# Gates of tiles 1 to 3 moved behind the attention, gates and output projection on operands in two parts

## The chip, the cores and the metric

One core of a Trainium2 chip runs the program. The metric is the device time of one execution in microseconds (us); a lower one is better. The kernel before takes 2186.17 us, the median of three runs (2179.91 to 2187.29). A difference of about 0.3%, some 6.6 us, is what a measurement of this kernel can tell from none.

## The reference, cut to what matters

Two layers follow each other on 512 tokens of width 1024. The first mixes two kinds of attention through gates, then adds a layer of experts that are looked up per token; the second is a state-space layer. The change lies in the first:

```
h = rmsnorm(x, norm1_g); proj = h @ w_in
qa, ka, va, qb, kb, vb, ga, gb = split(proj)
ya = neighbourhood_attention(qa, ka, va, rpb)          # 8 heads of 64
yb = gqa_attention(rope(norm(qb)), rope(norm(kb)), vb) # 8 heads of 64, 2 key heads
merged = sigmoid(ga) * (ya @ w_proj_a) + sigmoid(gb) * (yb @ w_proj_b)
x = x + merged @ w_out
x = x + peer(rmsnorm(x, norm2_g))     # per token 128 rows of peer_u and peer_v, 16 for each of 8 heads
...                                   # then the second layer
```

`ga` and `gb` are 1024 wide each, so the gates are two products of 512x1024 by 1024x1024. The kernel uses sigmoid(a) = (tanh(a/2) + 1) / 2. `peer` picks for each token and head 16 of 16384 experts by two rankings, and weights their rows.

## The kernel before

The tokens are four tiles of 128. Tile 0 goes first through attention, gates and output (`mix_first`), and its experts are ranked (`queries`, `ranked`, `best`). Tiles 1 to 3 then go together, 384 tokens wide, through `mix_rest`: `mixers` runs 24 units (2 kinds of attention, 4 pairs of heads, 3 tiles), and each unit is scores `s`, a softmax on VectorE and ScalarE, transposes `pT` and the weighted sum `y`. `beside(u)` is called behind each unit and, in this kernel, `spread` computes one 128-wide piece of a gate in it: pieces of `ga` behind units 0 to 7 (into `mT`), of `gb` behind units 12 to 19 (into the tile `gb`). `merge` then multiplies the attention's output `yT` by `wproj` (tile `pj`), multiplies it with the gates (L681, L682) and projects with `wout` (tile `xo`, L688). All of this is in fp32: a matmul of fp32 operands shows as two records in the trace.

The experts are the other half of the program. For each of the 4 x 128 experts of a tile's tokens, GpSimd gathers 128 rows of 8 KB (`uv`, L273) into one of six buffers `g`, VectorE multiplies and sums (L275), ScalarE applies Gelu (L280), VectorE builds a diagonal `dg` (L284) and, for tile 0, adds half of the output itself in `own` (L299, with L293), and TensorE adds the rest into `acc` (L289). A buffer `g` is free for the next gather when `acc` and `own` have read it. These steps are issued by a generator (`peers`) of two gathers a step: `Paced` counts the columns of every matmul (four for each fp32 column, one for one of fp32r) and, each time PACE columns have been issued, lets the generator take one step. PACE_B holds during `mix_rest` and the queries of tile 1, PACE_Q and PACE_C afterwards. The generator for tile 1 waits for the ranking of tile 1, which needs the result of `mix_rest`.

A scheduler then fixes the order on each engine. Each engine runs its instructions in that order, so what stands ahead of an `acc` on TensorE, or ahead of an L275 on VectorE, holds it up. After `mix_rest` come the queries of tile 1 (`pq`, `sc`) with a ranking behind each of four steps, then the queries and rankings of tiles 2 and 3, then the second layer for tiles 0 and 1 beside the last gathers, and for tiles 2 and 3 when all gathers are done.

Other places of the program already use operands in two parts: `halves` splits a weight tile into `ww`, a rounded fp32r part (a ScalarE cast, L357) and the rest (a VectorE subtraction, L358), and PARTS makes three fp32r products of it, high by high, high by low and low by high, each one record in the trace:

```
PARTS = ((0, 0), (0, 1), (1, 0))
A.copy(ww[:, 0], w)
V.tensor_tensor(ww[:, 1], w, ww[:, 0], op=OP.subtract)
```

Of the kernel before, what the change touches and what calls it, by code (L numbers as in the profile page):

```python
# [8 lines left out]
F32 = mybir.dt.float32  # L9
F32R = mybir.dt.float32r  # L10
# [4 lines left out]
OP = mybir.AluOpType  # L15
# [158 lines left out]
def program(tc, a, out):  # L174
# [2 lines left out]
    T = Paced(nc.tensor)  # L177
    first, rest = [0], [1, 2, 3]
    NG = 256
    PACE_B, PACE_Q, PACE_C = 15000, 10500, 4600  # L180

    with ExitStack() as ctx:
        cst = ctx.enter_context(tc.tile_pool(name="cst", bufs=1))
# [14 lines left out]
        def bank(name, tag="mm"):  # L198
            if tag in turns:
                turn[tag] = turn.get(tag, -1) + 1  # L200
                tag = turns[tag][turn[tag] % len(turns[tag])]
            return ps.tile([P, 512], F32, tag=tag, name=name, bufs=2 if tag in ("mm", "sb") else 1)

        def wtile(src, n):
            t = wp.tile([P, 1024 // n, n], F32, tag="w", name="w")
            SP.dma_start(t, src)
            return t
# [183 lines left out]
        with pool("pa") as pa:  # L391
# [28 lines left out]
            with pool("ph") as ph:  # L420
# [76 lines left out]
                def mix_rest(tiles, hs):  # L497
                    n = len(tiles) * P
                    with pool("p2") as py:
                        yT = py.tile([P, 8, n], F32, tag="yT", name="yT")  # L500
                        mT = py.tile([P, 8, n], F32, tag="mT", name="mT")
                        gb = []

                        def gate(i, w, dst):
                            b = bank("ga")
                            rows(w[i], hs, b, n)
                            A.activation(dst[:, i, :], b[:, :n], AF.Tanh, scale=0.5)

                        def spread(u):

                            if u < 8:
                                gate(u, a["wga"], mT)
                            if 12 <= u < 20:
                                if not gb:
                                    gb.append(pa.tile([P, 8, n], F32, tag="kv", name="gb"))
                                gate(u - 12, a["wgb"], gb[0])

                        def put(i, b):
                            A.copy(yT[:, i, :n], b[:, :n])

                        with pool("p2a", 2) as pw:
                            mixers(pw, tiles, hs, put, spread)
                        merge(tiles, yT, mT, gb[0])

                def mix_first(hs, hl):

# [142 lines left out]
                            weigh(*units[u - ahead])  # L669
                            beside(u - ahead)  # L670

                def merge(tiles, yT, mT, gb):
                    n = len(tiles) * P
                    for d in range(8):
                        w = wtile(a["wproj"][d], P)
                        sg = mT[:, d, :], gb[:, d, :]
                        for j, o in enumerate(sg):
                            b = bank("pj", "sb")
                            for k in range(4):
                                T.matmul(b[:, :n], w[:, 4 * j + k, :], yT[:, 4 * j + k, :n], start=(k == 0), stop=(k == 3))  # L680
                            V.scalar_tensor_tensor(o, o, 1.0, b[:, :n], op0=OP.add, op1=OP.mult)  # L681
                        V.tensor_tensor(sg[0], sg[0], sg[1], op=OP.add)  # L682
                    for half in range(2):
                        bs = [bank("xo") for _ in tiles]
                        cols(bs, mT, [(i, a["wout"][half, i]) for i in range(4)])
                        for i, t in enumerate(tiles):
                            xs = xres[:, t, half * 512:(half + 1) * 512]
                            V.scalar_tensor_tensor(xs, bs[i], 0.5, xs, op0=OP.mult, op1=OP.add)  # L688
# [463 lines left out]
```

## Time and profile before

| | us |
|---|---|
| median of three runs | 2186.17 |
| the profiled execution | 2190.49 |
| its span, first to last instruction | 2188.6 |
| TensorE busy (10292 matmul records) | 1817.3 |
| VectorE busy | 1625.2 |
| ScalarE busy | 736.3 |
| GpSimd busy (512 gathers) | 590.6 |

The profiled execution is 4.3 us above the median, and 1.9 us of it lie around the span. Its program can be cut by places that every reader finds again: the units of `mixers` for tiles 1 to 3 run from about 293 us (the first gate product) to 610 us (the last `y`), `merge` until 711 us, the queries and rankings of tile 1 until 795 us, those of tiles 2 and 3 until about 1130 us; the last gather lands at about 1905 us, and what follows is the second layer of tiles 2 and 3 alone. A busy share is the busy time of an engine over a stretch. A wait names the engine and line that waited and what ended the wait.

### The profile page before, as it was taken

The page shows a single profiled execution, that of the slowest core. Times are in us where ns is not written, and L with a number is a line of the kernel's source. Part 1 is how long each engine was busy: PE and PEld are TensorE (multiplying, and loading weights), DVE is VectorE, ACT ScalarE, POOL GpSimd, SP SyncE. Part 2 cuts the span into 40 slices and gives each one's busy share as a digit, 9 for nine tenths or more (in the row PEclk, how much of TensorE's full clock was granted, in tenths as well). Part 3 has the DMA queues.
Part 4 walks back from the last instruction along what each step waited for, and adds up shares of the span by engine and source line. Part 5 has one row for each costly group of instructions (what it writes and reads, how often), then busy time and mean ns, then how long its engine had stood idle before and what let it go on. Part 6 is the DMA issues. An engine that isn't in the chain of part 4 may idle for free.

```text
span 2188.6 us, 29527 instructions
## 1 busy us (share of the span) xinstructions
PE 1817.3 (83%) x10292; PEld 1030.6 (47%) x10292; DVE 1625.2 (74%) x4007; ACT 736.3 (34%) x1471; POOL 590.6 (27%) x520
## 2 busy tenths in 40 slices
PE   7898779989999799555567987896899866699998
PEld 5666534444443765011114653462463311189996
DVE  5376987788786685998877887886775756688865
ACT  4364256566500431111122342421220310144543
POOL 0000232333332133443433334333433334200000
PEclk9999889999999899666678997897899976699999
DMA  6366979889897989999998999899999999743453
GB/s 215 111 215 218 365 274 348 345 330 363 336 376 271 340 339 382 421 408 395 410 389 317 418 363 407 329 418 420 402 415 418 414 369 421 328 152 120 136 191 116
DMA packets 127316, 711.71 MB, mean 325 GB/s; under 512 B 15168, under 2 KB 18752, under 8 KB 61248
## 3 DMA queue, kind: packets, MB, share of 16 engines
q0 software_dynamic: 73728, 536.90, 60.8%
q1 hardware_dynamic: 53440, 172.92, 22.6%
q8 instruction: 83, 1.36, 0.2%
q14 instruction: 65, 0.53, 0.1%
HBM read 707.67 MB, written 2.10 MB: 324 GB/s over the span
## 4 chain that ended last, share of the span: by engine, by line
PE 34%; DVE 26%; DMA 23%; ACT 8%; issue 6%; POOL 1%; another core or an unknown queue 0%; SPq 0%; DVEq 0%; ACTq 0%; POOLq 0%
DMA g<-in_uv,idx 20%; DVE g L275 10%; PE sc L168 6%; PE acc L289 4%; PE mix L168 4%; PE pq L168 3%; DVE dg L284 2%; PE z L168 2%; DVE own L299 2%; DVE ww L358 2%; PE pg L168 2%; PE xbc L168 2%; ACT L280 2%; POOL g L273 1%; PE xo L168 1%
## 5 line engine op out<-in xcount | busy, mean ns | idle before, releaser
L273 POOL DMA_INDIRECT g<-in_uv,idx x512 | 586.8, 1146 | 1290.6 <-PE acc L289 636.5
L289 PE MATMUL acc<-g,dg 64*64 64x512 f32 x3584 | 606.7, 748 | 242.6 <-DVE dg L284 214.1
L275 DVE SCALAR_TENSOR_TENSOR g<-g,xnp 128x1024 f32<-128x1024 f32 x512 | 625.1, 1221 | 179.5 <-DMA g<-in_uv,idx 177.3
L289 PEld LDWEIGHTS acc<-g,dg 64*64 64x64 f32 x3584 | 126.8, 156 | 589.8 <-DVE dg L284 428.2
L280 ACT ACTIVATE act<-act 128x1 f32<-128x1 f32 (+1 forms) x448 | 90.9, 203 | 922.7 <-DVE g L275 893.2
L358 DVE TENSOR_TENSOR ww<-w,ww 128x1024 fp32r<-128x1024 f32 x175 | 213.5, 1223 | 82.7 <-ACT ww L357 81.2
L284 DVE TENSOR_SCALAR dg<-two,act,gate 128x64 f32<-128x64 f32 x512 | 169.8, 349 | 118.9 <-ACT act L280 109.9
L357 ACT CAST ww<-w 128x1024 fp32r<-128x1024 f32 x175 | 182.1, 1045 | 162.1 <-PE sc L168 46.8
L168 PEld LDWEIGHTS sc<-hT,ww 128*128 128x128 f32 x1536 | 192.4, 195 | 54.5 <-issue 43.8
L168 PE MATMUL sc<-hT,ww 128*128 128x256 f32 x1536 | 209.2, 292 | 5.5 <-ACT fold L337 3.3
L168 PE MATMUL pq<-xT,w 128*128 128x128 f32 (+1 forms) x768 | 124.2, 320 | 4.7 <-ACT q L736 3.8
L168 PEld LDWEIGHTS pq<-xT,w 128*128 128x128 f32 x768 | 111.8, 198 | 18.3 <-ACT q L736 5.5
L299 DVE SCALAR_TENSOR_TENSOR own<-g,hid,own 128x512 f32<-128x512 f32 x127 | 95.2, 750 | 2.3
L168 PE MATMUL ga<-h,w 128*128 128x384 f32 x256 | 92.5, 511 | 2.4 <-DVE rot L415 2.4
L280 ACT ACT_TABLE_LOAD x60 | 77.0, 1283 | 16.0 <-DVE g L275 13.0
L168 PE MATMUL xbc<-hT,ww 128*128 128x256 f32 x480 | 65.0, 292 | 11.1 <-ACT ww L357 5.7
L168 PEld LDWEIGHTS xbc<-hT,ww 128*128 128x128 f32 x480 | 59.9, 194 | 25.6 <-issue 8.6
L168 PEld LDWEIGHTS ga<-h,w 128*128 128x128 f32 x256 | 48.4, 197 | 36.9 <-issue 7.8
L168 PE MATMUL q<-h,w 128*128 128x128 f32 (+1 forms) x256 | 60.8, 392 | 4.2 <-ACT rsq L411 4.2
L168 PE MATMUL mix<-w,ycat 128*128 128x512 f32 x128 | 61.7, 612 | 0.0
L168 PEld LDWEIGHTS z<-hT,ww 128*128 128x128 f32 x384 | 46.9, 190 | 12.2 <-issue 10.5
L168 PEld LDWEIGHTS q<-h,w 128*128 128x128 f32 x256 | 40.5, 198 | 23.9 <-ACT rsq L411 4.8
(337 smaller groups left out, 2256.2 us busy)
## 6 DMA issues: line engine op xcount, KB each, us to landing
w<-in_w SPq DMA_DIRECT2D x100, 512.0 KB
w<-in_wq SPq DMA_DIRECT2D x48, 512.0 KB
w<-in_wo SPq DMA_DIRECT2D x32, 512.0 KB
w<-in_wgm SPq DMA_DIRECT2D x16, 512.0 KB
w<-in_wout SPq DMA_DIRECT2D x16, 512.0 KB
g<-in_uv,idx POOLq DMA_INDIRECT x512
w<-in_wpg SPq DMA_DIRECT2D x16, 512.0 KB
w<-in_wqa SPq DMA_DIRECT2D x8, 512.0 KB
```

The costliest lines, as they stand in the source:

```text
L168: return self.count(max(n, 128) * (4 if rhs.dtype == F32 else 1), self.tensor.matmul(out, lhsT, rhs, **kw))
L273: G.indirect_dma_start(out=g.rearrange("p a d -> p (a d)"), out_offset=None, in_=a["uv"], in_offset=bass.IndirectOffsetOnAxis(ap=hk_idx[t] ...
L275: V.scalar_tensor_tensor(g[:, 0, :], g[:, 0, :], 1.0, xnp, op0=OP.mult, op1=OP.mult, accum_out=act[:, j % grp:j % grp + 1])
L280: A.activation(act[:, :grp], act[:, :grp], AF.Gelu)
L284: V.tensor_scalar(dg[:, m, :], two[:, 1, :], act[:, m:m + 1], gate[:, m:m + 1], op0=OP.mult, op1=OP.mult)
L289: T.tensor.matmul(acc[i][o, :], w, v, start=(e0 + j + 1 == grp), stop=(e0 + j + grp >= P), tile_position=(64 * i, 64 * m), skip_group_chec ...
L299: V.scalar_tensor_tensor(own, g[:, 1, HALVES[1]], hid[:, j:j + 1], own, op0=OP.mult, op1=OP.add)
L357: A.copy(ww[:, 0], w)
L358: V.tensor_tensor(ww[:, 1], w, ww[:, 0], op=OP.subtract)
```

## The change

`spread`, `gate` and the tile `gb` go. `mixers` gets an empty function for `beside`, so its units follow one another with nothing between but the steps of the experts. `merge` gets the normed input `hs` and does more:

- `parts` splits `hs` (8 pieces of 128x384: a cast on ScalarE, a subtraction on VectorE) into `hp` and `hpl`, and later the merged `mT` into `mp` and `mpl`. The low parts lie in the tile of the keys and values, the high parts in a pool that opens when the pool of `mixers` has closed.
- For each of eight pieces `d`, both gates are computed by `halves` and PARTS (2 x 24 fp32r matmuls of 384 columns), tanh goes into two small tiles `sg`, and `wproj` is used as before.
- `wout` is split by `halves` too (8 tiles), and 144 fp32r matmuls of 512 columns take the place of 48 fp32 ones; the three accumulators `xo` lie in banks of two kinds (`mm`, `sb`).
- PACE_B is 13700 and was 15000. By Paced's count, `mix_rest` had 798,720 columns and has 724,992 now, so 53.2 steps of the generator and now 52.9; but `mixers` had 602,112 of them and has 405,504 now, 40.1 steps and now 29.6.

The weights that are loaded, the gathers and all the rest are the same.

```diff
--- before.py
+++ after.py
@@ -177,7 +177,7 @@
     T = Paced(nc.tensor)
     first, rest = [0], [1, 2, 3]
     NG = 256
-    PACE_B, PACE_Q, PACE_C = 15000, 10500, 4600
+    PACE_B, PACE_Q, PACE_C = 13700, 10500, 4600
 
     with ExitStack() as ctx:
         cst = ctx.enter_context(tc.tile_pool(name="cst", bufs=1))
@@ -498,29 +498,13 @@
                     n = len(tiles) * P
                     with pool("p2") as py:
                         yT = py.tile([P, 8, n], F32, tag="yT", name="yT")
-                        mT = py.tile([P, 8, n], F32, tag="mT", name="mT")
-                        gb = []
-
-                        def gate(i, w, dst):
-                            b = bank("ga")
-                            rows(w[i], hs, b, n)
-                            A.activation(dst[:, i, :], b[:, :n], AF.Tanh, scale=0.5)
-
-                        def spread(u):
-
-                            if u < 8:
-                                gate(u, a["wga"], mT)
-                            if 12 <= u < 20:
-                                if not gb:
-                                    gb.append(pa.tile([P, 8, n], F32, tag="kv", name="gb"))
-                                gate(u - 12, a["wgb"], gb[0])
-
                         def put(i, b):
                             A.copy(yT[:, i, :n], b[:, :n])
 
                         with pool("p2a", 2) as pw:
-                            mixers(pw, tiles, hs, put, spread)
-                        merge(tiles, yT, mT, gb[0])
+                            mixers(pw, tiles, hs, put, lambda u: None)
+                        with pool("p2m", 2) as pm:
+                            merge(pm, tiles, yT, hs)
 
                 def mix_first(hs, hl):
 
@@ -669,20 +653,48 @@
                             weigh(*units[u - ahead])
                             beside(u - ahead)
 
-                def merge(tiles, yT, mT, gb):
+                def merge(pm, tiles, yT, hs):
+
                     n = len(tiles) * P
+
+                    def parts(src, name):
+                        hi = pm.tile([P, 8, n], F32R, tag="hi", name=name, bufs=1)
+                        lo = pa.tile([P, 8, n], F32R, tag="kv", name=name + "l")
+                        for k in range(8):
+                            A.copy(hi[:, k, :], src[:, k, :])
+                            V.tensor_tensor(lo[:, k, :], src[:, k, :], hi[:, k, :], op=OP.subtract)
+                        return hi, lo
+
+                    hp = parts(hs, "hp")
+                    mT = ph.tile([P, 8, n], F32, tag="h2", name="mT")
                     for d in range(8):
+                        sg = []
+                        for j, src in enumerate((a["wga"], a["wgb"])):
+                            w = halves(pm, wtile(src[d], P))
+                            b = bank("ga")
+                            for k in range(8):
+                                for x, y in PARTS:
+                                    T.matmul(b[:, :n], w[:, x, k, :], hp[y][:, k, :], start=(k + x + y == 0), stop=(k == 7 and x == 1))
+                            o = pm.tile([P, n], F32, tag=f"sg{j}", name="sg")
+                            A.activation(o, b[:, :n], AF.Tanh, scale=0.5)
+                            sg.append(o)
                         w = wtile(a["wproj"][d], P)
-                        sg = mT[:, d, :], gb[:, d, :]
                         for j, o in enumerate(sg):
                             b = bank("pj", "sb")
                             for k in range(4):
                                 T.matmul(b[:, :n], w[:, 4 * j + k, :], yT[:, 4 * j + k, :n], start=(k == 0), stop=(k == 3))
                             V.scalar_tensor_tensor(o, o, 1.0, b[:, :n], op0=OP.add, op1=OP.mult)
-                        V.tensor_tensor(sg[0], sg[0], sg[1], op=OP.add)
+                        V.tensor_tensor(mT[:, d, :], sg[0], sg[1], op=OP.add)
+                    mp = parts(mT, "mp")
                     for half in range(2):
-                        bs = [bank("xo") for _ in tiles]
-                        cols(bs, mT, [(i, a["wout"][half, i]) for i in range(4)])
+                        bs = [bank("xo", "mm" if i < 2 else "sb") for i in range(len(tiles))]
+                        for m in range(4):
+                            w = halves(pm, wtile(a["wout"][half, m], 512))
+                            for i, b in enumerate(bs):
+                                for j in range(2):
+                                    for x, y in PARTS:
+                                        T.matmul(b, mp[x][:, 2 * m + j, i * P:(i + 1) * P], w[:, y, j, :],
+                                                 start=(m + j + x + y == 0), stop=(m == 3 and j == 1 and x == 1))
                         for i, t in enumerate(tiles):
                             xs = xres[:, t, half * 512:(half + 1) * 512]
                             V.scalar_tensor_tensor(xs, bs[i], 0.5, xs, op0=OP.mult, op1=OP.add)
```

The order on each engine shifts with it. On TensorE, in the middle of `mixers` (kind 0: `s` scores, `pT` transposes, `y` weighted sums, `acc` the experts), before:

```order
L168 MATMUL y<-pT,kv 64x128
L168 MATMUL ga<-h_1502,w 128x384 x8
L168 MATMUL s<-kv,qT 128x512
L168 MATMUL y<-pT,kv 64x128 x7
L171 MATMUL pT<-idn,s 128x128 x4
L289 MATMUL acc<-g,dg 64x512 x2
```

and in the changed kernel:

```order
L168 MATMUL y<-pT,kv 64x128
L171 MATMUL pT<-idn,s 128x128 x4
L168 MATMUL s<-kv,qT 128x512 x2
L168 MATMUL y<-pT,kv 64x128 x7
L171 MATMUL pT<-idn,s 128x128 x4
L168 MATMUL s<-kv,qT 128x512
L289 MATMUL acc<-g,dg 64x512 x4
```

The gate products are gone from between the units. Two `acc` belong to a gather of tile 0. Ahead of the last `y` stood 200 of them, 100 gathers, and stand 160 now, 80 gathers; ahead of the last `xo` stood all 256, and stand 208 now, 104 gathers.

On VectorE, in the middle of `merge`, before (L681 and L682 are the merging):

```order
L682 TENSOR_TENSOR mT<-mT,gb 128x384
L681 SCALAR_TENSOR_TENSOR mT<-mT,pj 128x384
L275 SCALAR_TENSOR_TENSOR g,act<-g,xnp 128x1024
L284 TENSOR_SCALAR dg<-two,act,gate 128x64 x2
L293 TENSOR_TENSOR hid<-act,gate 128x2
L299 SCALAR_TENSOR_TENSOR own<-g,hid,own 128x512
L275 SCALAR_TENSOR_TENSOR g,act<-g,xnp 128x1024
L299 SCALAR_TENSOR_TENSOR own<-g,hid,own 128x512
L681 SCALAR_TENSOR_TENSOR gb<-gb,pj 128x384
```

and in the changed kernel (L686 and L687 are the merging now, L358 the split of a weight tile):

```order
L687 TENSOR_TENSOR mT<-sg 128x384
L358 TENSOR_TENSOR ww<-w,ww 128x1024 x2
L686 SCALAR_TENSOR_TENSOR sg<-sg,pj 128x384 x2
L687 TENSOR_TENSOR mT<-sg 128x384
L358 TENSOR_TENSOR ww<-w,ww 128x1024 x2
L686 SCALAR_TENSOR_TENSOR sg<-sg,pj 128x384
L275 SCALAR_TENSOR_TENSOR g,act<-g,xnp 128x1024
```

The experts' work has left the middle of `merge`: on TensorE no `acc` stands between the 72nd and the 264th gate product.

On VectorE, in the first ranking of tile 1 (MAX, MAX_INDEX and MATCH_REPLACE find the largest scores), before:

```order
L774 TENSOR_TENSOR cand<-v_4793 128x2x56
L747 MATCH_REPLACE sc<-v_4793,sc 128x128 x4
L748 MAX v_4793<-sc 128x8 x4
L749 MAX_INDEX i_4794<-v_4793,sc 128x8 x3
L777 TENSOR_TENSOR cand<-v_4793 128x2x8
```

and in the changed kernel:

```order
L786 TENSOR_TENSOR cand<-v_5272 128x2x56
L759 MATCH_REPLACE sc<-v_5272,sc 128x128
L275 SCALAR_TENSOR_TENSOR g,act<-g,xnp 128x1024
L759 MATCH_REPLACE sc<-v_5272,sc 128x128
L299 SCALAR_TENSOR_TENSOR own<-g,hid,own 128x512
L759 MATCH_REPLACE sc<-v_5272,sc 128x128 x2
L760 MAX v_5272<-sc 128x8 x2
```

Work on the last gathers of tile 0 has moved in between. From the last `xres` of `mix_rest` (L688) to the last indices of tile 1 (L812) VectorE handled 10 gathers, and handles 30 now; at those indices both orders stand at gather 138, and both go on alike from there.

## Rows read from the trace of the kernel before

**Rows 1.** Page, part 4: share of the span by engine, then by line, in the chain.
```profile
PE 34%; DVE 26%; DMA 23%; ACT 8%; issue 6%; POOL 1%; another core or an unknown queue 0%; SPq 0%; DVEq 0%; ACTq 0%; POOLq 0%
DMA g<-in_uv,idx 20%; DVE g L275 10%; PE sc L168 6%; PE acc L289 4%; PE mix L168 4%; PE pq L168 3%; DVE dg L284 2%; PE z L168 2%; DVE own L299 2%; DVE ww L358 2%; PE pg L168 2%; PE xbc L168 2%; ACT L280 2%; POOL g L273 1%; PE xo L168 1%
```

**Rows 2.** Busy time by stretch: us, busy us per engine, clock, DMA share, GB/s.
```profile
core 0: us, PE busy (x) PEld busy (x) DVE busy (x) ACT busy (x) POOL busy (x), PEclk, DMA share, GB/s
250.00:300.00 50.00, 34.51 (x114) 15.37 (x113) 48.21 (x200) 18.84 (x35) 14.02 (x10) 0.73 0.82 311
293.00:610.00 317.00, 292.53 (x1411) 143.29 (x1411) 247.88 (x553) 188.61 (x324) 102.34 (x89) 0.99 0.88 337
409.00:455.00 46.00, 35.86 (x218) 17.31 (x218) 37.80 (x83) 30.07 (x52) 16.43 (x15) 1.00 0.85 335
610.00:711.00 101.00, 94.75 (x328) 41.25 (x324) 75.11 (x151) 4.58 (x19) 26.67 (x24) 1.00 0.83 324
711.00:795.00 84.00, 70.08 (x478) 57.76 (x479) 65.90 (x331) 32.19 (x66) 20.41 (x18) 0.90 0.89 336
862.00:1120.00 258.00, 149.75 (x818) 31.89 (x810) 228.19 (x751) 37.56 (x139) 114.80 (x100) 0.68 0.99 408
```

**Rows 3.** Waits, 293 to 706 us: engine line waited for: us, times, longest us.
```profile
POOL g L273 <- PE acc L289: 192.2, 33, 13.7
...
DVE g L275 <- DMA g<-in_uv,idx: 44.6, 31, 3.7
```

**Rows 4.** GpSimd in order of time: start us, us, operation [idle before <-releaser].
```profile
686.12 1.43 POOL L273 DMA_INDIRECT g<-in_uv,idx  x1 [0.30 <-issue]
741.54 0.94 POOL L273 DMA_INDIRECT g<-in_uv,idx  x1 [53.99 <-issue]
```

**Rows 5.** TensorE in order of time: last mixing product, first query product behind.
```profile
609.41 1.09 PE L168 MATMUL y<-pT,vb 128*64 128x128 f32 x16
...
711.80 0.39 PE L168 MATMUL pq<-xT,w 128*128 128x128 f32 x2
```

**Rows 6.** VectorE in order of time: last indices of tile 1.
```profile
795.39 0.18 DVE L812 CAST idx<-idxf 128x32 int32<-128x32 f32 x1
```

**Rows 7.** Lines by shape, 293 to 706 us: xcount | busy us, mean ns | idle before.
```profile
L275 DVE SCALAR_TENSOR_TENSOR g<-g,xnp 128x1024 f32<-128x1024 f32 x115 | 140.3, 1220 | 44.6 <-DMA g<-in_uv,idx 44.6
...
L168 PE MATMUL ga<-h,w 128*128 128x384 f32 x256 | 92.5, 511 | 2.4 <-DVE rot L415 2.4
L299 DVE SCALAR_TENSOR_TENSOR own<-g,hid,own 128x512 f32<-128x512 f32 x118 | 88.5, 750 | 2.3
L289 PE MATMUL acc<-g,dg 64*64 64x512 f32 x468 | 74.0, 611 | 9.3 <-DVE dg L284 7.5 <-DVE hid L293 1.8
...
L168 PE MATMUL pj<-yT,w 128*128 128x384 f32 x128 | 44.0, 494 | 3.0 <-DVE gb L681 3.0
...
L284 DVE TENSOR_SCALAR dg<-two,act,gate 128x64 f32<-128x64 f32 x116 | 31.9, 336 | 29.4 <-ACT act L280 28.3 <-issue 1.0
...
L275 DVE DVE_READ_ACCUMULATOR g<-g,xnp 128x1 f32 x115 | 9.6, 84 | 0.0
L293 DVE TENSOR_TENSOR hid<-act,gate 128x2 f32<-128x2 f32 x58 | 9.1, 157 | 0.0
```

**Rows 8.** Lines by shape, 1950 to 2150 us, where operands are in two parts.
```profile
L168 PE MATMUL sc<-hT,ww 128*128 128x256 f32 x768 | 96.2, 285 | 0.0
...
L358 DVE TENSOR_TENSOR ww<-w,ww 128x1024 fp32r<-128x1024 f32 x59 | 72.2, 1224 | 29.0 <-ACT ww L357 28.6
L357 ACT CAST ww<-w 128x1024 fp32r<-128x1024 f32 x58 | 60.7, 1046 | 71.6 <-PE sc L168 33.4 <-PE mix L168 19.0 <-issue 11.7
L168 PE MATMUL mix<-ww,yc 128*128 128x512 f32 x180 | 41.6, 393 | 0.0
```

## The prediction

> **What bounds the kernel now.** I read the chain first [rows 1]: no engine holds more than a third of it, TensorE 34%, VectorE 26%, transfers 23%, and the longest single item is the landing of gathers, 20%. So the program is a long queue of gathers, and what matters is how fast the rest lets them go. Busy time by stretch says which engine that is [rows 2]. From 293 to 610 us, where the change takes its gates out, TensorE is busy 292.53 of 317 us, 92%; VectorE 78%, ScalarE 59%. From 610 to 711 us, the merging, TensorE is busy 94%. From 862 to 1120 us it is VectorE, 88%, with the DMA engines at 0.99. The waits say how the gathers hang on this [rows 3]: GpSimd waited 192.2 us for an `acc` on TensorE to free a buffer, while VectorE waited 44.6 us for gathers. TensorE is thus the bound in front, but VectorE is close behind. One hole stands out: the last gather of tile 0 is issued at 686.12 us, the next one at 741.54 us, when tile 1's first indices are there [rows 4]. I cut the program at the last `y` (610 us), the first query product of tile 1 (711 us) [rows 5] and tile 1's last indices (795 us) [rows 6]. At the last of these both orders stand at gather 138, so what the change costs up to there should be what it costs in all: behind it the work is the same, with the DMA engines full until 1120 us, and I see nothing that gives time back.
>
> **What a gather of tile 0 costs.** On VectorE 1220 + 84 + 336 + 750 + half of 157 ns, 2.47 us. On TensorE two `acc` of two records, 74.0 us for 468 records being 158 ns each, 0.63 us [rows 7].
>
> **First stretch, the attention.** The change takes out the gates, 256 records and 92.5 us of TensorE [rows 7], and the order takes out 20 gathers (80 instead of 100 ahead of the last `y`). TensorE falls from 292.5 to 292.5 - 92.5 - 12.6 = 187 us. VectorE falls from 247.9 by 20 x 2.47 to 198.5 us. TensorE is then no longer the bound; without gates to fill in, softmax, transposes and experts wait for each other, and VectorE is the longest. The trace holds a piece of such work: from 409 to 455 us no gate product but those at its end ran, and VectorE was busy 82%, TensorE 78% [rows 2]. There the experts came thicker, so I take 85%: 198.5 / 0.85 = 233.5 us instead of 317, a gain of 83.5 us. Its bounds are 78%, VectorE's share in this stretch now (254 us, a gain of 63), and 88%, that of 862 to 1120 us (224.5 us, a gain of 92.5). [...]
>
> **Second stretch, the merging.** It was 101 us. The gates arrive, 384 fp32r products of 384 columns. The trace has such products of 256 columns, 96.2 us for 768, 125 ns, and of 512, 41.6 us for 180, 231 ns [rows 8]; I take the middle, 178 ns, 68.4 us, with 48 and 89 us as bounds. `wproj` took 44.0 us for 64 products [rows 7], of which 56 stand behind the last `y`, 38.5 us. The output becomes 144 products of 231 ns, 33.3 us. With 24 gathers of 0.63 us, 15.1 us, TensorE has 155 us. In front of it the split of `hs` must run, which can begin only when the pool of `mixers` is closed: 8 pieces that no row shows, at most 1.22 us each like a whole split [rows 8] and at least nothing for all but the first; I take 5 us. In the output VectorE has eight splits of 1.22 us and ten gathers, 34.5 us, with the low parts of `mT` and the additions to `xres` on top, as much as TensorE's 33.3 + 6.3 us, and a split that stands behind a gather waits for its landing; I take 8 us, between 0 and 20. That makes 168 us, 67 us more. The rest is covered: 24 weight splits are 24 x 1.05 = 25 us on ScalarE, which was busy 4.58 of 101 us here, and 24 x 1.22 = 29 us on VectorE, which with 24 gathers (59 us) stays far under 168. If that cover failed, each gate would wait about 2.3 us, 37 us for 16. The 16 weight tiles of the gates change their place on SP's queue too: 8.4 MB at the 408 GB/s of 862 to 1120 us [rows 2] are 21 us, beside 24 gathers, which came at 258 / 100 = 2.58 us each from 862 us on, 62 us; the DMA engines have room. But gathers starve here: no `acc` stands between the 72nd and 264th gate product.
>
> **Third stretch, tile 1's rankings.** VectorE was busy 65.9 of 84 us [rows 2]. The 20 gathers that were left behind come here, 49.4 us, so it has 115.3 us. At 88%, its share from 862 us on, where rankings and gathers also mix, that is 130 us, 46 us more. Were it never idle, 31 us more; at the share it has here now, 78%, 63 us more. The gathers fill the hole after 686 us, which helps the DMA engines, but VectorE was at work in it.
>
> **The sum.** -83.5 + 67 + 46 = +29.5 us on the profiled execution's 2190.5 us, 2220 us; that execution was 4.3 us over the median, so 2216 us. In words: TensorE saves some 35 us of products, VectorE gets 24 x 1.22 us and the small splits more, and work that lay side by side is put into one stretch that only TensorE fills and one that only VectorE fills.
>
> **Rivals.** *VectorE packs (faster).* With fewer gathers among the units and none of tile 0 waiting behind gates, VectorE could run at the 96% of 250 to 300 us [rows 2], 48.21 of 50 us, in the first and third stretch. Then they take 207 and 120 us, gains and costs of 110 and 36; with the 13 us of waits in the merging gone too (54 us more) the sum is -20 us, 2166 us. It gets faster by over 0.3% from a share of 92%: (198.5 + 115.3) / 0.92 = 341, 60 us under the 401 now, against 54. For it speaks that VectorE's idle time is mostly waits for gathers (44.6 us) which come thinner; against it that at 96% nothing of attention ran beside.
> *It comes out even.* The 20 gathers first fill the 18 us in which VectorE is idle in the third stretch, and it is then never idle (31 us more); the attention runs at 88% (a gain of 92.5), the merging at half its waits (61 us more). Sum 0, 2186 us.
> *The clock falls.* If the attention gets the 0.73 of 250 to 300 us, TensorE needs 187 / 0.73 = 257 us there, and at its own 92% of now 278 us, 44.5 us more than forecast: 2260 us. For it speaks the row at 69% busy, against it the one at 78%; the forecast has TensorE at 187 / 233.5 = 80%.
>
> **How the numbers follow.** The forecast has 0.53: it rests on two counted sums and on shares of VectorE of which this trace has nearby examples. Packing 0.22, even 0.13, the clock 0.12. Some 0.3%, 6.6 us, is what can be told from no change. Slower: nearly all of the forecast (0.49) and the clock, 0.61. Faster: nearly all of packing and a rest of the forecast, 0.23. Within: 0.16. By its bounds the forecast goes from -92.5 + 54 + 31 = -7 us to -63 + 87 + 63 = +87 us; its ends need all bounds at once. The range from 2172 to 2250 us takes in the even case and most of packing, and leaves out the clock case and packing's far end.
>
> **What would show it.** In the profile of the changed kernel the last `y` should end near 527 us, the first query product of tile 1 start near 695, tile 1's last indices come near 825. VectorE should be busy about 85% up to the last `y`, TensorE over 90% in the merging, VectorE about 88% in the rankings, and gathers should be few in the merging and without a hole behind it. A gate product should take near 178 ns. The prediction is wrong if the attention ends before about 505 us, if the rankings cost under 35 us more, or if the shift at the last indices is not the shift at the end.

## The result, and the profile after

The changed kernel takes 2220.5 us, the median of six runs (2211.49 to 2222.79), beside 2186.73 us for the kernel before on the same chip: a ratio of 1.0155, 95% interval 1.0136 to 1.0174. The forecast was 2216 us, slower. The profiled execution of the changed kernel took 2222.79 us, its span is 2221.0 us, 32.4 us more than before.

The chain of waits, page part 4 (shares of the span by engine, then by line), answers to [rows 1]: still no engine above some 36%, and transfers of gathers the longest item.

```profile
PE 36%; DVE 24%; DMA 20%; issue 9%; ACT 8%; POOL 2%; POOLq 0%; SPq 0%; DVEq 0%; ACTq 0%
DMA g<-in_uv,idx 18%; DVE g L275 9%; PE sc L168 6%; PE acc L289 4%; PE ga L168 3%; POOL g L273 2%; PE mix L168 2%; DVE dg L284 2%; PE z L168 2%; PE pj L168 2%; PE pg L168 2%; DVE ww L358 2%; PE xo L168 2%; ACT L280 2%; PE xbc L168 2%
```

The three places at which the prediction cut the program, in order of time: the last `y` and the end of the output on TensorE, tile 1's last indices on VectorE [rows 5, 6].

```profile
529.58 1.09 PE L168 MATMUL y<-pT,vb 128*64 128x128 f32 x14
...
694.64 0.39 PE L168 MATMUL xo<-ww,mpl 128*128 128x512 f32 x1
...
817.06 0.17 DVE L824 CAST idx<-idxf 128x32 int32<-128x32 f32 x1
```

The busy time by stretch, cut there, answers to [rows 2] (columns as there: us, busy us and instructions of each engine, granted clock, DMA share, GB/s). The last two rows cut the whole program at 1150 us.

```profile
core 0: us, PE busy (x) PEld busy (x) DVE busy (x) ACT busy (x) POOL busy (x), PEclk, DMA share, GB/s
293.00:531.00 238.00, 208.05 (x1068) 96.52 (x1066) 197.64 (x449) 173.99 (x293) 76.69 (x68) 0.92 0.86 318
531.00:695.00 164.00, 159.81 (x742) 120.09 (x742) 109.68 (x193) 40.09 (x71) 32.41 (x27) 0.98 0.74 278
695.00:817.00 122.00, 95.19 (x539) 66.29 (x539) 111.34 (x426) 39.85 (x84) 38.60 (x32) 0.85 0.92 362
862.00:1120.00 258.00, 154.70 (x862) 41.16 (x864) 220.41 (x752) 39.50 (x146) 118.76 (x99) 0.71 0.99 404
0.00:1150.00 1150.00, 925.11 (x4768) 535.74 (x4768) 876.01 (x2482) 440.21 (x855) 310.91 (x267) 0.87 0.83 315
1150.00:1900.00 750.00, 616.73 (x3710) 298.84 (x3714) 549.42 (x1115) 195.04 (x447) 279.34 (x243) 0.86 0.97 395
```

The same first 1150 us of the kernel before:

```profile
0.00:1150.00 1150.00, 928.87 (x4704) 498.67 (x4704) 868.99 (x2493) 421.13 (x838) 313.64 (x278) 0.89 0.85 326
```

The engines did about as much by 1150 us as before; what differs is the bytes: 315 instead of 326 GB/s, 12.7 MB less in 1150 us. The DMA engines are nearly full from 862 us on (a share of 0.99 until 1120 us and of 0.97 from 1150 to 1900 us), so what was not moved in time is moved later: 12.7 MB at 405 GB/s are 31 us, and the span is 32.4 us longer. The 405 GB/s are an estimate of what the full DMA engines move, from the 404 to 408 GB/s at a share of 0.99 (862 to 1120 us, changed kernel and kernel before). No run shows the most that they can move; the highest stretch of 150 us read here has 418 GB/s (750 to 900 us, changed kernel at pace 11500, at a share of 1.01).

Where the bytes were lost, the order of time on GpSimd shows (start, us, operation, idle before it and what ended that); it answers to [rows 4]:

```profile
554.19 1.47 POOL L273 DMA_INDIRECT g<-in_uv,idx  x1 [1.87 <-DVE mT L687]
614.11 0.94 POOL L273 DMA_INDIRECT g<-in_uv,idx  x1 [58.45 <-PE acc L289]
```

The 54 us hole in front of tile 1's indices is gone, and one of 58 us stands in the merging. TensorE ran gate and `wproj` products there and no `acc` between 554 and 612 us, so the six buffers stayed full (the DMA share of these 58 us is 0.48, 166 GB/s). The old hole was made up for in part when it ended: tile 1's gathers have four buffers more (a pool `gx` of their own), and before the change ten of them were issued in a row from 741.54 us on. The waits of GpSimd from 293 to 700 us, beside [rows 3]:

```profile
POOL g L273 <- PE acc L289: 172.3, 24, 58.5
...
DVE g L275 <- DMA g<-in_uv,idx: 16.3, 12, 4.4
```

The sum of the waits for `acc` is below the 192.2 us of before; new is the one long wait, 58.5 us, where the longest was 13.7. From 293 to 700 us GpSimd issued 95 gathers, and 112 before the change.

### The profile page after: what moved, and what is told of

Read it like the earlier page. It is cut to its first block, busy times and chain, and to the rows that moved or that the text cites. A ratio compares the mean times of both kernels' runs of the same rounds, so it can differ in the third digit from the quotient of the medians.

```text
span 2221.0 us, 30015 instructions
## 1 busy us (share of the span) xinstructions
PE 1836.1 (83%) x10468; PEld 1076.3 (48%) x10468; DVE 1657.1 (75%) x4047; ACT 770.4 (35%) x1516; POOL 601.3 (27%) x520
## 3 DMA queue, kind: packets, MB, share of 16 engines
q0 software_dynamic: 73728, 536.90, 60.1%
## 4 chain that ended last, share of the span: by engine, by line
PE 36%; DVE 24%; DMA 20%; issue 9%; ACT 8%; POOL 2%; POOLq 0%; SPq 0%; DVEq 0%; ACTq 0%
DMA g<-in_uv,idx 18%; DVE g L275 9%; PE sc L168 6%; PE acc L289 4%; PE ga L168 3%; POOL g L273 2%; PE mix L168 2%; DVE dg L284 2%; PE z L168 2%; PE pj L168 2%; PE pg L168 2%; DVE ww L358 2%; PE xo L168 2%; ACT L280 2%; PE xbc L168 2%
## 5 line engine op out<-in xcount | busy, mean ns | idle before, releaser
L273 POOL DMA_INDIRECT g<-in_uv,idx x512 | 597.5, 1167 | 1311.2 <-PE acc L289 656.2
L289 PE MATMUL acc<-g,dg 64*64 64x512 f32 x3584 | 629.3, 755 | 262.3 <-DVE dg L284 244.9
L358 DVE TENSOR_TENSOR ww<-w,ww 128x1024 fp32r<-128x1024 f32 x199 | 242.6, 1222 | 103.0 <-ACT ww L357 101.6
L357 ACT CAST ww<-w 128x1024 fp32r<-128x1024 f32 x199 | 207.1, 1044 | 168.0 <-PE sc L168 46.9
L168 PEld LDWEIGHTS sc<-hT,ww 128*128 128x128 f32 x1536 | 191.8, 194 | 54.8 <-issue 43.9
L168 PE MATMUL pq<-xT,w 128*128 128x128 f32 (+1 forms) x768 | 129.4, 328 | 1.7 <-ACT q L748 1.7
L168 PE MATMUL ga<-hp,ww 128*128 128x384 f32 x256 | 71.7, 356 | 4.0 <-ACT ww L357 3.3
L168 PE MATMUL q<-h,w 128*128 128x128 f32 (+1 forms) x256 | 66.9, 417 | 3.9 <-ACT rsq L411 3.9
L168 PEld LDWEIGHTS ga<-hp,ww 128*128 128x128 f32 x256 | 47.7, 194 | 10.0 <-ACT ww L357 5.2
```

What stands on the lines that cost most here:

```text
L168: return self.count(max(n, 128) * (4 if rhs.dtype == F32 else 1), self.tensor.matmul(out, lhsT, rhs, **kw))
L273: G.indirect_dma_start(out=g.rearrange("p a d -> p (a d)"), out_offset=None, in_=a["uv"], in_offset=bass.IndirectOffsetOnAxis(ap=hk_idx[t] ...
L289: T.tensor.matmul(acc[i][o, :], w, v, start=(e0 + j + 1 == grp), stop=(e0 + j + grp >= P), tile_position=(64 * i, 64 * m), skip_group_chec ...
```

## The experiments

Each states the ratio to the kernel before on the same chip, with its 95% interval. One chip ran the first four runs, the same one the next four, another the last four; the kernel before took 2181.4, 2184.1 and 2178.5 us there.

**The pace of the steps alone, and the place of the gates alone.** The change holds three things: where the gates stand, two parts, and the pace. The first run is the kernel before with the new pace only:

```diff
-    PACE_B, PACE_Q, PACE_C = 15000, 10500, 4600
+    PACE_B, PACE_Q, PACE_C = 13700, 10500, 4600
```

> The kernel before with PACE_B at 13700, nothing else. Theory (the change is slower because the gates left the attention and the experts then starve in the merging): the order up to the last output product has the same gathers as before (100 ahead of the last mixing product, 128 ahead of the last output product), so 2187 us, between 2178 and 2195. Rival (the pace itself costs): more than 2200 us.

Measured: 2184.36 us, 1.0022 [1.0005, 1.0039]. In the kernel before, this pace by itself does next to nothing. The second run moves the gates and leaves everything in fp32, with the pace at its old 15000:

```diff
-                            mixers(pw, tiles, hs, put, spread)
-                        merge(tiles, yT, mT, gb[0])
+                            mixers(pw, tiles, hs, put, lambda u: None)
+                        with pool("p2m", 2) as pm:
+                            merge(pm, tiles, yT, hs)
...
+                            b = bank("ga")
+                            rows(src[d], hs, b, n)
```

> Gates moved behind the attention, but gates and output stay in fp32 and PACE_B at 15000, so nothing is split. Theory: the attention ends near 531 us as in the changed kernel, the merging takes about 92.5 + 38.5 + 43 + 30 gathers of 0.63 us and some waits, 195 to 205 us, so the first query product comes near 730 us, the rankings cost what they cost in the changed kernel, and the whole comes to 2250 us (2235 to 2265): the two parts give back, the move alone costs. Rival (the splits, 33 us more on VectorE and 33 us on ScalarE, make the change slow): without them 2190 us or less.

Measured: 2253.98 us, 1.0333 [1.0301, 1.0366]. So the move alone costs some 73 us at that pace, and the changed kernel by its ratio 34. The 39 us between them are about what the two parts take off TensorE: 128 fp32 products of the gates, 92.5 us [rows 7], become 384 of 174 ns, 66.8 us, and the output, 96 records of 43.2 us in all, becomes 144 products 231 ns apart, 33 us. That the two parts give them back is not shown by this pair, because the pace differs too, and the next runs show that the pace of the moved kernel can be worth as much.

**Another pace for the changed kernel.**

```diff
-    PACE_B, PACE_Q, PACE_C = 13700, 10500, 4600
+    PACE_B, PACE_Q, PACE_C = 11500, 10500, 4600
```

> The changed kernel with PACE_B at 11500 instead of 13700. Its order has 80 gathers ahead of the last mixing product as the changed kernel, but 122 instead of 104 ahead of the last output product, and no stretch of the merging without experts longer than about 19 us of TensorE work. Theory (the gathers that are put off are what costs): attention to about 531 us, merging 175 to 185 us instead of 164, rankings back to about 85 to 95 us, and 2195 us in all (2183 to 2207). Rival (what costs is the added work of the splits, or the attention alone without gates): 2220 us, as the changed kernel.

Measured: 2184.27 us, 1.0021 [1.0001, 1.0040], at the low end of what was expected; the rankings took 102 us, not 85 to 95. With nothing changed but the pace, all but some 5 us of the loss is gone. The products and the splits are the same as in the changed kernel. GpSimd's longest wait in the merging is 15 us, and the first 1150 us read:

```profile
0.00:1150.00 1150.00, 924.29 (x4869) 533.93 (x4869) 896.13 (x2530) 446.04 (x874) 320.62 (x278) 0.88 0.84 326
```

These are the 326 GB/s of the kernel before. It is no rule about a thicker pace, though. At 10500 and at 12500:

> The changed kernel with PACE_B at 10500. Its order has 90 gathers ahead of the last mixing product and all 128 ahead of the last output product. Theory: as the run at 11500, since VectorE has the same work to do until the rankings of tiles 2 and 3 are done, 2184 us (2174 to 2194). Rival (the sooner the gathers, the better): each of the 6 to 10 gathers that come earlier is worth 2.58 us, 2165 us.

> The changed kernel with the steps of the experts set at 12500 instead of 13700. Theory A: the loss goes with the MB that are not moved by 1150 us, end = 2186 + (375.2 - MB) / 0.405 within 6 us; the longest stretch of TensorE's order without an expert's product is 38 us (61 at 13700, 19 at 11500 which cost nothing): 2195 to 2205. Rival (moving the gates costs its 30 us whatever the pace, and 11500 was a lucky order): 2215 to 2225.

Measured: 2212.48 us, 1.0121 [1.0090, 1.0152], and 2206.92 us, 1.0147 [1.0115, 1.0179]; both expectations fell (at 12500 the time is just above the expected 2205, but its ratio is that of the rival). At 12500 GpSimd waits twice for long for an `acc`, 37 us in the merging and 41 us in tile 1's rankings. At 10500 its longest wait in the merging is 23 us, but there is a hole in front of tile 1's indices, where tile 0's gathers had run out 62 us before:

```profile
769.96 0.94 POOL L273 DMA_INDIRECT g<-in_uv,idx  x1 [59.93 <-PE pq L168]
```

A hole in that place is no sign of loss by itself: the kernel before has one of 54 us there [rows 4], and the run at 11500, which loses next to nothing, one of 32 us:

```profile
734.48 0.94 POOL L273 DMA_INDIRECT g<-in_uv,idx  x1 [32.46 <-PE pq L168]
```

What differs here is when it ends: at 770 us, against 742 and 734. At 10500 the last `y` came at 563 us, at 11500 at 527; ten gathers more stand ahead of it at 10500, and the granted clock from 293 us up to it was 0.88 and not 0.95. Which of the two made the attention longer, no run separates. The length of the longest stretch of TensorE's order without an `acc`, on which the last expectation leaned, is a poor sign of the loss.

**Is TensorE's time in the attention worth anything?** Two runs leave the gates' products out of the kernel before, at two paces:

```diff
-                            b = bank("ga")
-                            rows(w[i], hs, b, n)
-                            A.activation(dst[:, i, :], b[:, :n], AF.Tanh, scale=0.5)
+                            V.memset(dst[:, i, :], 0.0)
```

> The kernel before without its two gate products for tiles 1 to 3 (tanh of them is set to zero by small VectorE writes, so the output is not the reference's), PACE_B at 13700: 92.5 us of TensorE work are gone and nothing takes their place. Theory (VectorE limits the attention once the gates are gone, and the gathers left behind come back in the rankings): the attention ends near 530 us, a gain of 80 us, but the rankings cost some 40 us more and a few gathers are missing in flight, so 2150 us (2138 to 2165). Rival (TensorE is the bound through and through): the whole 92 us are saved, 2095 us.

> The kernel without the two gate products for tiles 1 to 3 (their tanh set to zero, so the output is not the reference's) once more, with PACE_B at 11360, which gives the generator the same 53 steps in mix_rest as the kernel before had; the run before gave it 43.9 of them by the same count. Its order stands at gather 138 at tile 1's last indices, as before and as the changed kernel. Theory (TensorE's 92.5 us have a price only as far as VectorE lets the gathers follow; what cost in the run without gates was the steps that went with the columns): faster than the kernel before, 2155 us (2140 to 2172). Rival (work on TensorE in the attention is wholly covered): 2182 us, as before. Other rival (TensorE the bound): 2095 us.

Measured: 2200.18 us, 1.0095 [1.0075, 1.0114], at 13700, and 2181.88 us, 0.9985 [0.9961, 1.0009], at 11360, where as many steps fall into the stretch as before. The second is the run that decided most: 92.5 us of TensorE and 8.4 MB of loads are gone, the last `y` comes 66 us earlier (544 instead of 610 us), and nothing that can be told from no change is left of it at the end. The expected 2150 and 2155 us were missed, and of the rivals the one of 2182 us came about. The idea that TensorE is the bound in front and its time there comes back fell with it. The first 1150 us at 11360:

```profile
0.00:1150.00 1150.00, 887.58 (x4532) 471.78 (x4533) 885.48 (x2535) 422.71 (x838) 323.13 (x283) 0.86 0.84 324
```

At 13700 the kernel is even slower for doing less. Fewer steps fall into the stretch (43.9 instead of 53), and GpSimd stood still for 83 us, from 720 to 803 us:

```profile
803.25 0.94 POOL L273 DMA_INDIRECT g<-in_uv,idx  x1 [82.89 <-PE acc L289]
```

But by 1150 us it had issued 270 gathers, as many as the kernel before, so gathers put off up to there do not explain this loss; its cause stays open.

**What is a gather worth that is put off?** The kernel before with a thinner pace (19500 for 15000):

> The kernel before with PACE_B at 19500 instead of 15000: no work added, removed or moved but the steps of the experts, of which 12 gathers fewer stand ahead of tile 1's last indices in VectorE's order (126 instead of 138). Theory (gathers put off are paid for at about 2.58 us each, since the stretch to 1120 us has no room to make them up): 12 x 2.58 = 31 us more, 2212 us (2203 to 2222), with the attention and the merging ending a little earlier than before. Rival (gathers put off are made up for later, the loss of the changed kernel comes from its work): 2182 us.

Measured: 2207.77 us, 1.0107 [1.0078, 1.0137]; nothing was added but distance between the steps, and it costs 24 us. That lies in the expected range, at 8 gathers fewer by 1150 us (262 instead of 270) and not 12.

**Half of the move.** Gate `ga` stays in the attention in fp32, in every third unit; `gb` and the output stand behind it in two parts, at a pace of 12300.

> Half of the move: the pieces of the first gate stay in the attention, in fp32, one behind every third unit; the second gate is computed behind it on operands in two parts, and the output projection too; PACE_B at 12300. Its order has 90 gathers ahead of the last mixing product and 120 ahead of the last output product, with no stretch without experts of over 17 us of TensorE work. Theory (the cost is gathers put off, and TensorE's saving is worth little because VectorE limits the whole up to 1120 us): 2182 us as before (2172 to 2192). Rival (each moved gate costs by itself): halfway to the changed kernel, 2198 us.

Measured: 2210.93 us, 1.0119 [1.0094, 1.0145]; above both expected values. Its attention takes as long as before, 605 us to the last `y`, but GpSimd waits in it nine times for 10 to 18 us (before, six times for 10 to 14), and the rate from 300 to 600 us is 283 to 301 GB/s against 336 to 345. The granted clock is lower there too, 0.86 from 293 to 606 us against 0.99 from 293 to 610, and no run tells what of the loss is due to that.

**Are the DMA engines the bound?** By now one number went along with the time in every run: the bytes moved by 1150 us. To test that and not only watch it, 16 loads of 512 KB (8.4 MB) into a tile that nobody reads were added, once late in the kernel before, for the most part where the DMA engines are full (a share of 0.99 from 862 to 1120 us), and once in the merging of the changed one, where they are not (0.74).

```diff
                         b = bank("pq")
+                        if len(tiles) == 2:
+                            SP.dma_start(pw.tile([P, 8, P], F32, tag="spare", name="spare", bufs=1), a["wq"][2 * h0 + j])
                         rows(a["wq"][2 * h0 + j], xT[:, :, t0:t0 + m], b, m)
```

> The kernel before with 16 extra loads of 512 KB (8.4 MB) into a tile that nobody reads, one beside each weight tile of the queries of tiles 2 and 3, behind tile 1's last indices (after about 800 us), where the DMA share of the kernel before is 0.94 to 0.98. Theory A (from about 750 us on the 16 DMA engines set the end, at about 405 GB/s, and whatever is not moved before then is paid later): 8.4 MB / 405 GB/s = 20.7 us more, 2207 us beside 2186. Theory B (VectorE, 88% busy between 860 and 1120 us, sets the end, and the transfers are only queued behind it): no more than 5 us, below 2191.

```diff
                             w = halves(pm, wtile(src[d], P))
+                            SP.dma_start(pm.tile([P, 8, P], F32, tag="spare", name="spare", bufs=1), src[d])
                             b = bank("ga")
```

> The changed kernel with the same 16 extra loads of 512 KB (8.4 MB), one behind each gate's weight tile in the merging (531 to 695 us), where its DMA share is 0.74 against 0.91 of the kernel before in the same stretch (278 against 360 GB/s over 164 us, 13.4 MB less). Theory A (only bytes that are not moved in time count, and these travel while the DMA engines stand idle): 0 to 5 us above the changed kernel, 2220 to 2226, ratio 1.015 to 1.018. Theory A' (every byte costs wherever it is put): 20.7 us, 2241, ratio 1.025. Theory B (the DMA engines do not matter): 2220, so this run by itself tells A from A' only, and A from B together with the loads behind the indices.

Measured: the late loads 2194.02 us, 1.0078 [1.0053, 1.0103], 17 us more (11.5 to 22.4), which holds the 20.7 us of the full DMA engines and excludes the 5 us of VectorE as the bound. Three of the 16 went out ahead of tile 1's last indices, at 743, 761 and 774 us, and ten between 860 and 936 us. The delay can be read from the trace: from the 146th to the 230th gather it takes 258 us, against 247 in the kernel before and 237 in the run of the pace alone. It is no wait for weights behind the added loads: `pq` waited 0.8 us for its weights in all. The row beside [rows 2]:

```profile
862.00:1120.00 258.00, 148.68 (x778) 30.33 (x775) 222.76 (x727) 37.52 (x136) 109.32 (x94) 0.66 1.00 412
```

The loads in the merging, one at 485 us and 15 from 539 to 612 us, 2215.9 us, 1.0178 [1.0144, 1.0212]; beside the 1.0155 of the changed kernel that is 5 us more (-3.5 to 13.6, the two intervals combined), which excludes 20.7. The merging of that run, with the changed kernel's clock, lengths and VectorE time:

```profile
531.00:695.00 164.00, 159.93 (x757) 119.78 (x756) 109.66 (x195) 40.04 (x70) 32.67 (x27) 0.98 0.88 330
```

330 instead of 278 GB/s are the 8.5 MB, in the same 164 us. So the same bytes cost 17 us where the DMA engines are mostly full and 5 us in the hole, which its interval does not tell from nothing; the 12 us between the two have an interval of 2 to 22.

**The output alone in two parts**, gates left where they were:

```diff
-                        bs = [bank("xo") for _ in tiles]
-                        cols(bs, mT, [(i, a["wout"][half, i]) for i in range(4)])
+                        bs = [bank("xo", "mm" if i < 2 else "sb") for i in range(len(tiles))]
+                        for m in range(4):
+                            w = halves(pm, wtile(a["wout"][half, m], 512))
...
```

> The kernel before with the output product alone in two parts (gates stay in the attention, fp32). It takes about 36 us of TensorE off the merging, and adds the 5 us split of the merged rows. Theory A: TensorE time as such is worth nothing; what counts is the MB moved by 1150 us (375.2 in the kernel before, 362.2 in the changed one), end = 2186 + (375.2 - MB) / 0.405, within 6 us. The longest stretch of TensorE's order without an expert's product is 36 us (changed kernel 61, the one at pace 11500 19), so between the two: 2184 to 2200. Rival (the TensorE time taken off the merging comes back at the end): 2186 - 31 = 2155.

Measured: 2167.23 us, 0.9945 [0.9920, 0.9969], 12 us (7 to 17) faster than the kernel before on its chip. It fell below the 2184 to 2200 expected from the order. The 36 us that were named as taken off TensorE were wrong too: the output had 43.2 us in the kernel before (lines by shape, 606 to 712 us) and takes 33, so 10 us, and the rival priced with them was no fair one.

```profile
L168 PE MATMUL xo<-w,mT 128*128 128x512 f32 x96 | 43.2, 600 | 3.2 <-DMA w<-in_wout 1.9 <-DVE xres L688 1.3
```

The run cannot tell whether those 10 us come back as such or through the gathers, since its rate by 1150 us is higher as well (276 gathers instead of 270):

```profile
0.00:1150.00 1150.00, 940.36 (x4852) 518.75 (x4852) 896.39 (x2539) 441.12 (x869) 318.83 (x284) 0.88 0.86 333
```

**All runs beside the bytes.** GB/s are those of the first 1150 us; MB behind are (326 - GB/s) x 1.15, less the 8.4 MB that a run has to move less (no gates) and more the 8.4 MB that it has to move more (loads); the shift by bytes is that over 405 GB/s, and the shift of the span is the span less 2188.6 us, both of the profiled executions. The shift by ratio is what the ratio makes of the median of the kernel before on the run's own chip. Gathers are those issued by 1150 us, 270 in the kernel before. A rate is rounded to 1 GB/s, which is 3 us, and the chips differ by up to 8 us in the kernel before, of which only the first has a profile here. Two profiled executions lie off their medians: the one without gates at 11360, 2171.72 us, 10 us below, and the one at pace 10500, 2220.67 us, 8 us above.

```
run                        GB/s  MB behind  by bytes  of the span  by ratio  gathers
changed kernel              315     12.7      +31        +32         +34       259
pace alone                  326      0          0         -8          +5       270
moved, fp32                 306     23        +57        +63         +73       250
changed, pace 11500         326      0          0         -9          +5       270
no gates, 13700             318      0.8       +2         +6         +21       270
no gates, 11360             324     -6.1      -15        -19          -3       275
before, pace 19500          320      6.9      +17        +20         +23       262
half moved                  319      8.1      +20        +23         +26       262
changed, pace 10500         319      8.1      +20        +30         +26       262
late loads                  333      0.4       +1         +4         +17       270
changed, loads in merging   323     11.9      +29        +24         +39       260
output in two parts         333     -8.1      -20        -25         -12       276
changed, pace 12500         318      9.2      +23        +15         +32       262
```

From -25 to +63 us the bytes give every span within 10 us. By the ratio, every run lies 3 to 19 us above the bytes: part of that can be the span they are set beside, since the profiled execution of the kernel before is 4 us over its median and its chip the slowest of the three. Most is missing at the run without gates at 13700 (19 us), the moved one in fp32 and the late loads (16 each). So the bytes order the large shifts and do not read finer than some 15 us.

The gathers say the same more closely. From 1150 us to the last one they were issued 3.03 to 3.10 us apart on average in every run, and from there to the end of the span it took 292 to 298 us. The changed kernel had 11 fewer out by 1150 us, 34 us at 3.06 each; its span grew by 32.4. The run without gates at 13700, which the bytes do not explain, has the slowest gathers behind 1150 us (3.10).

The table by itself only goes along with the time, since three quarters of the bytes are gathers (536.90 of 711.71 MB); the two runs with loads are what shows that bytes, and not VectorE, hold up the stretch behind the indices; for the time behind 1150 us, only the share of 0.97 speaks for it.

## Why the prediction was right, step by step

**Attention: held.** 238 us instead of the forecast 233.5. VectorE was busy 197.64 us (198.5) at 83% (85%). TensorE had 208 us, not 187. Its granted clock was 0.92 and not 0.99, and 187 x 0.99 / 0.92 = 201, so by this estimate the clock makes 14 of the 21 us, and the rest is open. That is the clock rival in small: thinner work went with a lower clock here, 0.92 at TensorE 87% busy beside 0.99 at 92% before. It did not from 409 to 455 us of the kernel before, 1.00 at 78% [rows 2], and no run shows what sets the clock. Nor was TensorE, 87% busy, shown to set the end of this stretch.

**Merging: held.** 164 us instead of 168; TensorE was busy 97%. The gate products stand 174 ns apart (178), as from 554.48 to 561.63 us, 41 of them in 7.15 us. The lines by shape, 293 to 700 us (xcount | busy us, mean ns; the two groups of products overlap in time, so their busy times do not add), answer to [rows 7, 8]:

```profile
L168 PE MATMUL ga<-hp,ww 128*128 128x384 f32 x256 | 71.7, 356 | 4.0 <-ACT ww L357 3.3 <-DVE ww L358 0.6
...
L168 PE MATMUL ga<-hpl,ww 128*128 128x384 f32 x128 | 44.2, 345 | 0.0
...
L358 DVE TENSOR_TENSOR ww<-w,ww 128x1024 fp32r<-128x1024 f32 x24 | 29.2, 1220 | 27.9 <-ACT ww L357 27.9
...
L665 DVE TENSOR_TENSOR hpl<-h,hp 128x384 fp32r<-128x384 f32 x8 | 3.9, 545 | 0.0
```

The split of `hs`, bounded from above by 1.22 us a piece, takes 0.55 us. The gate products on TensorE waited 4.0 us for split weights in all, so the splits were covered as forecast. The ends of the range, -7 and +87 us, took in only part of the bounds given for this stretch (gates at 48 or 89 us and the waits at their ends make it some 35 to 105 us longer, not 54 to 87); as it came 63 us longer, that did not matter.

**Rankings: a little too dear.** 122 us instead of 130; VectorE was busy 111.3 us (115.3) and at 91%, not 88%; each of the two makes some 4 of the 8 us. That the share rose because 20 more gathers stand between the rankings is likely and not shown.

**The shift at the last indices is the shift at the end: failed.** This was the third of the prediction's own signs of being wrong. The shift is 21.7 us there (29.5 forecast) and 32.4 us at the end. Both orders stand at gather 138 on VectorE at that place, but GpSimd does not: before, with the ten issued in a row from 741.54 us on, 146 gathers were out at the indices; now 142. Four gathers at the 2.58 us of the stretch behind are 10 us, and 21.7 + 10 = 32. The three terms erred by 4.5 us too little (attention), 4 too much (merging) and 8 too much (rankings), and the step left out 10. That the sum still came out only 2.9 us below the measured end is luck: the errors cancel.

**The reason given: only half right.** The prediction said that TensorE saves little and that the loss is work of TensorE and of VectorE no longer lying side by side. That the gathers starve in the merging it saw, and it gave that no price of its own. The runs give the price to gathers that come late: the changed kernel at 11500 keeps the moved work, has as many gathers out by 1150 us as before and loses some 5 us, and 92.5 us less TensorE in the attention gain nothing. At 13700 the wait of 58 us in the merging is what makes them late; at 10500 the loss comes without such a wait, from tile 1's indices being late. Reading "TensorE is the bound in front" from its 92% [rows 2] was the weak place; a share of 0.83 to 0.89 on the DMA engines, with 0.99 behind, was the row that decided. That the hole behind 686 us moves was seen too; that a hole is worth its own bytes was not.

**The rivals.** VectorE did not pack to 92% in front (83% and 91%). That it comes out even happened at 11500, not here. What stays open is why the order starves the gathers in the merging at 12500 and 13700 and not at 11500, and whether more buffers would bridge the wait, which no run tried.

## What to carry to other kernels

Where one resource is full in the second half of a program, look at what it did not carry in the first: here a hole of 58 us there was paid for behind it, by its bytes and gathers (12.7 MB and 11 gathers fewer by 1150 us, a span 32.4 us longer), whatever the engines gained meanwhile. Price a moved block not only by its own time but by how long it keeps the instructions out of an in-order queue that free the buffers of a stream (here no `acc` for 58 us); then try several distances for that stream before judging the block. Operands in two parts paid 12 us for the output alone, where no gate changed its place; with the gates moved as well, the kernel lost 26 to 34 us at three of its four paces and some 5 at the fourth.

## What the runs showed that was not expected

- Leaving out 92.5 us of TensorE made the kernel slower by 1% at one pace and left it as it was at another; at 11500 instead of 13700 the changed kernel is 29 us faster by the ratios, and at 10500 and 12500 by no more than the noise (7 and 2 us).
- The 16 DMA engines moved 398 to 411 GB/s from 900 to 1150 us in the nine of the fourteen traces with a share of 0.98 to 1.00 there, and 418 from 750 to 900 us in two, at 1.01 and 1.02.
- The added loads of 512 KB took 4.3 to 4.4 us from issue to landing in the merging, at a DMA share of 0.88, and 9.8 us (medians) in the run of the late loads, at a share of 1.02 from 750 to 900 us and of 0.98 from 900 to 1150 us.
